# A hybrid layer's attention: the sum of exponentials by the tensor engine, value products in 65 columns, negated scores, and memory scores with 67 rows

## The chip, the core and the metric

The kernel runs on one core of a Trainium2 chip. The metric is the device time of one execution in microseconds (us). The core has a tensor engine (PE, whose weight loads are shown apart as PEld), a vector engine (DVE), a scalar engine (ACT), GpSimd (POOL) and a queue that issues DMAs (SP). PE writes its products to PSUM; POOL has no way to read PSUM.

## The reference, cut to what is computed

```python
D_MODEL, SEQ, HEAD_DIM, FOX_HEADS, MEM_HEADS, N_MEM = 1024, 2048, 64, 8, 4, 256

def fox_attention(q, k, v, logf):            # (B, H, S, 64), causal
    F = jnp.cumsum(logf, axis=-1)
    ...
    logits = einsum('bhqd,bhkd->bhqk', qi, k) * scale
    logits = logits + Fi[..., None] - F[:, :, None, :]
    logits = jnp.where(causal, logits, -1e30)
    p = jax.nn.softmax(logits, axis=-1)
    return einsum('bhqk,bhkd->bhqd', p, v)

def memory_attention(q, k, v):               # every query reads 256 memory tokens
    p = jax.nn.softmax(einsum('bhqd,bhmd->bhqm', q, k) * scale, axis=-1)
    return einsum('bhqm,bhmd->bhqd', p, v)

def reference(x, mem, ...):
    h = rms_norm(x, norm_g)
    u_a, g_a, q_b, k_b, v_b, f_b, g_b, q_m, g_m = split_cols(h @ w_in)
    y_a = pool_mixer(u_a, w_pool, pool_scale)
    y_b = fox_attention(rms_norm(q_b), rms_norm(k_b), v_b, log_sigmoid(f_b + b_f))
    y_m = memory_attention(rms_norm(q_m), rms_norm(k_m), v_m)
    mixed = concatenate([y_a * silu(g_a), y_b * silu(g_b), y_m * silu(g_m)])
    return x + mixed @ w_out
```

## The kernel before

The layer is cut into 16 units `n`: four groups `p` of heads (two forgetting-attention heads, one memory head, 64 pooled columns each) by four blocks `j` of 512 queries. For each unit PE first makes the input projection (`pa`, `pb` tiles, line 711), then the attention. At the end comes the output projection (`po`, also line 711). All operands are pairs of fp16 numbers, a high and a low part, so that one product takes three matmuls.

Attention of one head goes through these steps, with the queries on the partitions:

- `scores` (line 1113): q times k into a PSUM tile `qk` of 1024 columns, two matmuls per piece, line 1135 with the high parts and line 1140 with both parts. In the forgetting heads the first has 67 rows: 64 of the head, and three that carry the forget sums, against three rows of constants in `Q`. In the memory head (`h == 2`) it has 64 rows. Line 1138 adds the causal mask.
- `soften` (line 1144): DVE takes each row's largest score (line 1156) and its negative (line 1159); ACT makes the exponentials `p` and, through `accum_out`, their sum per row (line 1168; the second instruction is an ACTIVATION_READ_ACCUMULATOR).
- `weights` (line 1179): the factor of each part of the keys. There are two parts (`g` 0 and 1, of 1024 keys each) for `j` of 2 and 3, and one otherwise and in the memory head. POOL, ACT and DVE work on tiny tiles of up to 8 columns here, ending in a reciprocal of the sum.
- `halves` (line 1212): `p` as a high half `ph` (a cast, on ACT at line 1221 or DVE at line 1218) and a low half (a subtraction, line 1225, on DVE or POOL), and a DMA transpose to `pt` (line 1231), which puts the keys on the partitions. There are 336 such transposes.
- `weigh` (line 1236): for each block of 128 queries by 128 keys two matmuls into `pv`, of 128 columns (line 1260: high half by low and high part of the values) and 64 columns (line 1261: low half by high part), each with its own weight load.
- `gather`, `part`, `finish` (lines 1270 to 1317): DVE adds the two 64-column halves of `pv` (line 1277), scales by the factor (line 1311 four times per head, or 1300 and 1306 with two parts) and multiplies into the gate.

What sets the order is the class `Order`: a clock with a plain model of the engines (`COST`, and the costs that each step yields or gives to `use`). Each step runs when the model says that its operands are there; `sooner` picks the engine that would be done first. So one changed cost or step moves instructions everywhere, and which engine makes a high or a low half is decided anew. On the chip each engine then runs its instructions in this order. PSUM has two `qk` tiles and two `pv` tiles; seven subpieces may lie between scores and weighing (`DEEP`).

Of the kernel before, what the change touches and what calls it, by code (L numbers as in the profile page):

```python
# [10 lines left out]
F32 = mybir.dt.float32  # L11
F16 = mybir.dt.float16
# [22 lines left out]
NEG = -1e30  # L35
# [12 lines left out]
class Order:  # L48
    """Program order.  Processes are generators; each yields the tensor engine's time of what it has
    just emitted, or a negative time to be left alone for that long.  The clock follows a plain model  # L50
    of the engines, so that every engine's queue is filled in the order in which operands become ready."""
# [23 lines left out]
    def use(self, eng, n, fixed=None):  # L75
        """accounts for an instruction that has been emitted; returns when others see its result"""
# [34 lines left out]
    def claim(self, place):  # L111
        """waits for what has been reserved"""
# [30 lines left out]
    def merged(self, *streams):  # L143
        """Interleaves generators of given cost; each runs from fraction f0 to f1 of the whole."""
# [16 lines left out]
    def pair(self, lead, follow, lag):  # L161
        """Runs two generators of (unit, cost) on the tensor engine; follow's unit is kept lag behind lead's."""
# [23 lines left out]
def units(gen, start, total, span=1.0):  # L186
    """pairs each cost of gen with how far it has come, from start to start + span"""
# [11 lines left out]
class Layer:  # L199
    DEEP = 7  # score pieces in flight between the two products of the attention  # L200
# [1090 lines left out]
    def finish(self, n, h, head):  # L1291
# [23 lines left out]
        if g:  # L1315
            o.give(ft)
# [312 lines left out]
```

## Time and profile before

| what | value |
|---|---|
| device time, median of 3 runs | 1102.77 us (1100.82 to 1104.7) |
| span of the profiled execution, first to last instruction | 1095.0 us |
| busy: PE, DVE, ACT, POOL | 999.5, 852.6, 608.4, 468.3 us |
| granted PE clock, mean of the span | 0.981 of full |

The profile gives the span of its execution and no other time of it; the median of the runs is 7.8 us longer than that span. The chain of waits goes back from the last instruction, at each step to what released it. A busy PE may still be waiting inside, since matmuls overlap: how far apart two matmuls start tells more than how long one is said to take.

### The profile page before, as it was taken

To read this page: it belongs to the slowest core of one execution; us is meant where nothing else is said; L and a number is where in the kernel's file an instruction comes from. 1 tells how busy PE (TensorE), PEld (TensorE's weight loads), DVE (VectorE), ACT (ScalarE), POOL (GpSimd) and SP (SyncE) were. 2 spreads that over 40 slices of the span, in tenths; PEclk is the share of its full clock that TensorE was granted. 3 is DMA by queue.
4 is the path that set the end of the run, shared out by engine and by line. 5 is a ranking of instruction groups with operands and counts; after the bars stand their busy time and mean duration, and the time that the engine had idled before them with its cause. 6 is when DMAs were issued, how large, how long until landed. Compare 5 with 4: busy or idle time off the path is not lost.

```text
span 1095.0 us, 21836 instructions
## 1 busy us (share of the span) xinstructions
PE 999.5 (91%) x7477; PEld 588.6 (54%) x7477; DVE 852.6 (78%) x2059; ACT 608.4 (56%) x1867; POOL 468.3 (43%) x554
## 2 busy tenths in 40 slices
PE   6799899979899999998999898989899979999998
PEld 3356555546556555555565555555556644554443
DVE  6977887688998997987987979889978797872111
ACT  4776666576757466666664667476556564440000
POOL 5643453254545454545435446564535463220000
PEclk9899998999999999999999999999999999999999
DMA  9999999999999998998999969999989799998531
GB/s 273 229 220 211 219 247 252 254 149 177 180 208 205 216 209 189 188 169 165 206 205 222 205 148 206 199 216 203 194 227 214 158 169 254 226 234 213 196 104 48
DMA packets 485694, 219.20 MB, mean 200 GB/s; under 512 B 442128, under 2 KB 450256, under 8 KB 484560
## 3 DMA queue, kind: packets, MB, share of 16 engines
q1 hardware_dynamic: 485440, 217.81, 91.4%
q8 instruction: 58, 0.95, 0.4%
q14 instruction: 52, 0.43, 0.1%
q10 hardware_dynamic: 144, 0.01, 0.0%
HBM read 84.23 MB, written 25.26 MB: 100 GB/s over the span
## 4 chain that ended last, share of the span: by engine, by line
PE 40%; DVE 26%; DMA 16%; ACT 7%; issue 6%; POOL 4%; SPq 2%; ACTq 0%; POOLq 0%; DVEq 0%
PE po L711 14%; DMA pt<-ph 12%; PE pa L711 10%; DVE mx L1156 5%; PE pb L711 5%; DVE ph L1225 3%; ACT p L1168 3%; PE q L1135 2%; PE q L1140 2%; PE pv L1260 2%; DVE gate L1311 2%; DVE ph L1218 2%; DMA xx<-k 2%; POOL rr L966 1%; DVE hy L1277 1%
## 5 line engine op out<-in xcount | busy, mean ns | idle before, releaser
L1168 ACT ACTIVATE p<-q,nm 128x512 f32<-128x512 f32 (+3 forms) x384 | 228.8, 602 | 168.0 <-DVE nm L1159 105.0
L711 PEld LDWEIGHTS <-x 128*128 128x128 f16 x2304 | 215.9, 99 | 136.6 <-issue 4.5
L1225 POOL TENSOR_TENSOR ph<-p,ph 128x512 f16<-128x512 f32 (+3 forms) x153 | 174.2, 1144 | 218.5 <-ACT ph L1221 101.7
L711 PE MATMUL pa<-ah,x 128*128 128x512 f16 x768 | 250.3, 382 | 2.0 <-DVE z L941 2.0
L1156 DVE TENSOR_REDUCE mx<-q 128x1 f32<-128x128 f32 (+2 forms) x192 | 171.1, 905 | 10.4 <-PE q L1140 10.2
L1260 PE MATMUL pv<-v,pt 128*128 128x128 f16 x1088 | 132.4, 221 | 35.2 <-DMA pt<-ph 34.8
L711 PE MATMUL po<-aho,om 128*128 128x512 f16 x512 | 160.3, 382 | 0.0
L1260 PEld LDWEIGHTS <-pt 128*128 128x128 f16 x1216 | 110.5, 98 | 74.0 <-DMA pt<-ph 57.0
L711 PE MATMUL pa<-al,x 128*128 128x512 f16 x384 | 147.0, 383 | 0.0
L711 PE MATMUL pb<-bh,x 128*128 128x256 f16 x768 | 144.5, 275 | 2.5 <-ACT sq L932 1.0
L1221 ACT CAST ph<-p 128x512 f16<-128x512 f32 (+3 forms) x198 | 113.3, 585 | 38.9 <-DMA pt<-ph 28.9
L1225 DVE TENSOR_TENSOR ph<-p,ph 128x512 f16<-128x512 f32 (+3 forms) x183 | 125.4, 694 | 7.5 <-ACT ph L1221 5.2
L1135 PE MATMUL q<-k,q 67*128 67x512 f16 (+2 forms) x320 | 111.3, 350 | 19.4 <-ACT p L1168 17.6
L1261 PE MATMUL pv<-v,pt 128*128 128x64 f16 x1088 | 124.2, 193 | 0.0
L711 PEld LDWEIGHTS <-om 128*128 128x128 f16 x768 | 73.7, 99 | 84.5 <-issue 3.0
L1261 PEld LDWEIGHTS <-pt 128*128 128x128 f16 x1216 | 107.6, 98 | 20.3 <-issue 1.1
L966 POOL TENSOR_TENSOR rr<-ss,mhalf 128x10 f32<-128x10 f32 x32 | 64.6, 2018 | 121.8 <-DVE ss L961 106.7
L1140 PE MATMUL q<-k,q 128*128 128x512 f16 (+2 forms) x320 | 111.0, 349 | 0.0
L711 PE MATMUL pb<-bl,x 128*128 128x256 f16 x384 | 105.5, 275 | 0.0
L711 PE MATMUL po<-alo,om 128*128 128x512 f16 x256 | 97.8, 382 | 0.0
L711 PEld LDWEIGHTS <-xx 128*128 128x128 f16 x720 | 70.0, 100 | 51.5 <-issue 7.4
L1493 DVE SCALAR_TENSOR_TENSOR xo<-po,So_p,xo 128x512 f32<-128x512 f32 x32 | 23.9, 748 | 87.1 <-PE po L711 87.1
(245 smaller groups left out, 1762.7 us busy)
## 6 DMA issues: line engine op xcount, KB each, us to landing
x<-xd SPq DMA_DIRECT2D x48, 512.0 KB, 5.6
xrx<-in_x SPq DMA_DIRECT2D x16, 512.0 KB, 4.4
xd<-xx SPq DMA_DIRECT2D x16, 512.0 KB, 9.4
md<-mt SPq DMA_DIRECT2D x32, 256.0 KB, 3.5
om<-md SPq DMA_DIRECT2D x8, 1024.0 KB, 6.7
xo<-in_x SPq DMA_DIRECT2D x16, 512.0 KB, 3.8
out_dram<-xo SPq DMA_DIRECT2D x32, 256.0 KB, 3.9
w0a<-in_w_a SPq DMA_DIRECT2D x12, 512.0 KB, 5.2
```

The lines of the kernel that those rows point to most:

```text
L711: nc.tensor.matmul(out, rows, r[kt][:, :ncol], start=(kt == 0 and i == 0), stop=(kt == KT - 1 and i == 2))
L966: nc.gpsimd.tensor_tensor(rr, ss, self.mhalf[:, 0:10].rearrange("p (a b) -> p a b", b=5), op=ALU.pow)
L1135: nc.tensor.matmul(out, q1, kb, start=bank not in used, stop=False, **kw)
L1140: nc.tensor.matmul(out, q2, ka, start=False, stop=True, **kw)
L1156: nc.vector.tensor_reduce(mx[:, g, i:i + 1], qk[:, off:off + w], axis=AX.X, op=ALU.max)
L1168: nc.scalar.activation(p32[:, at:at + w], qk[:, off:off + w], AF.Exp, bias=nm[:, g, i:i + 1], accum_out=head["ls"][:, g, part, i:i + 1])
L1218: nc.vector.tensor_copy(hl[:, :w], p32[:, :w])
L1221: nc.scalar.copy(hl[:, :w], p32[:, :w])
L1225: (nc.vector if eng == "V" else nc.gpsimd).tensor_tensor(hl[:, w:2 * w], p32[:, :w], hl[:, :w], op=ALU.subtract)
L1260: nc.tensor.matmul(pv[:, i, :], ph, v, start=start and b == 0, stop=False, **kw)
L1261: nc.tensor.matmul(pv[:, i, HD:], pl, v[:, HD:], start=False, stop=end and b == nb - 1, **kw)
L1493: nc.vector.scalar_tensor_tensor(xr[:, t, :], pj, self.So, xr[:, t, :], op0=ALU.mult, op1=ALU.add)
```

## The change

The exponentials' sum is no longer made by ACT. Each values tile gets one more column, a constant of 2^14 behind the high part (`VW` is 132 columns per head of which 129 are used), so that PE's product of exponentials and values gives the sum in column 64. The value product of a block is now three matmuls into the same 65 columns: high half by [high part, constant], high half by low part (64 columns), low half by [high part, constant]. So `gather`, which added two halves, and `weights` are gone. `pv` has 65 columns per query block in place of 128.

The scores are negated (the gains and the constant rows of `Q` change sign), so DVE takes the smallest, and ACT's exponential has a scale of -1. The second part of the keys uses the smaller of the two parts' values, so that only the first part needs a factor, one `exp` of a difference (`al`). The memory scores read three more rows, which are zero in the keys.

At the end of a head DVE takes the reciprocal of column 64 and multiplies by it, straight from PSUM where there is one part. The product with the gate is always POOL's. `hy` has three buffers in place of two; some costs of the model change (the exponential's, a value block's); the scratch for dynamic DMA descriptors is set to 1024 bytes.

```diff
-            v = kv.tile([P, 4, 2, P], F16, name=f"v{i}")
+            self.V.append(kv.tile([P, 4, 2, VW], F16, name=f"v{i}"))
...
+        for v in [*self.V, self.Vm]:
+            nc.gpsimd.memset(v[:, :, :, 2 * HD:2 * HD + 1], ONE)
...
+            nc.gpsimd.memset(self.Km[HD:HD + 3, 0], 0.0)
...
-        r = HD + 3 if h < 2 else HD
+        r = HD + 3
...
-                nc.vector.tensor_reduce(mx[:, g, i:i + 1], qk[:, off:off + w], axis=AX.X, op=ALU.max)
+                nc.vector.tensor_reduce(mn[:, g, i:i + 1], qk[:, off:off + w], axis=AX.X, op=ALU.min)
...
-        nc.vector.tensor_scalar(nm[:, g, i0:i1], mx[:, g, i0:i1], -1.0, LN_P, op0=ALU.mult, op1=ALU.add)
+        if g:
+            nc.vector.scalar_tensor_tensor(
+                nm[:, 1, i0:i1], mn[:, 1, i0:i1], LN_P, nm[:, 0, i0:i1], op0=ALU.add, op1=ALU.min
+            )
+        else:
+            nc.vector.tensor_scalar(nm[:, 0, i0:i1], mn[:, 0, i0:i1], LN_P, None, op0=ALU.add)
...
-                    p32[:, at:at + w], qk[:, off:off + w], AF.Exp, bias=nm[:, g, i:i + 1], accum_out=head["ls"][:, g, part, i:i + 1]
-                t = o.use("A", 1.1 * w + 140)
+                nc.scalar.activation(p32[:, at:at + w], qk[:, off:off + w], AF.Exp, bias=nm[:, g, i:i + 1], scale=-1.0)
+                t = o.use("A", 1.0 * w + 180)
...
-            yield from self.weights(n, h, g, head)
+        if g and i1 == 4:
+            al = head["al"] = self.sm.tile([P, 4], F32, tag="al", bufs=3, name=f"al{n}{h}")
+            nc.gpsimd.tensor_tensor(al, nm[:, 1, :], nm[:, 0, :], op=ALU.subtract)
+            yield from o.at(o.use("G", 0, 0.3))
             nc.scalar.activation(al, al, AF.Exp)
...
-                nc.tensor.matmul(pv[:, i, :], ph, v, start=start and b == 0, stop=False, **kw)
-                nc.tensor.matmul(pv[:, i, HD:], pl, v[:, HD:], start=False, stop=end and b == nb - 1, **kw)
+                hi = v[:, HD:2 * HD + 1]
+                nc.tensor.matmul(pv[:, i, :], ph, hi, start=start and b == 0, stop=False, **kw)
+                nc.tensor.matmul(pv[:, i, 0:HD], ph, v[:, 0:HD], start=False, stop=False, **kw)
+                nc.tensor.matmul(pv[:, i, :], pl, hi, start=False, stop=end and b == nb - 1, **kw)
...
-                    yield 0.0856 * (2 - b % 2)
+                    yield 0.0885 * (2 - b % 2)
...
     def part(self, n, h, head):
...
+        yield from o.until(lambda: "scaled" in head)
+        nc.vector.tensor_tensor(y, pv, head["al"].unsqueeze(2).broadcast_to([P, 4, HD + 1]), op=ALU.mult)
...
     def finish(self, n, h, head):
...
+            nc.vector.tensor_tensor(y, y, pv, op=ALU.add)
...
+        nc.vector.reciprocal(rs, src[:, :, HD])
+        nc.vector.scalar_tensor_tensor(
+            y[:, :, 0:HD], src[:, :, 0:HD], 2.0 ** -29 * ONE, rs.unsqueeze(2).broadcast_to([P, 4, HD]), op0=ALU.mult, op1=ALU.mult
+        )
...
+        for u in range(2):
+            gate = head["gates"][u][0][:, :, c0:c0 + HD]
+            nc.gpsimd.tensor_tensor(gate, gate, y[:, 2 * u:2 * u + 2, 0:HD], op=ALU.mult)
```

In numbers of instructions, over the whole program: PE gets 1216 more matmuls and as many more weight loads. The low halves (`ph<-p,ph`) stand 221 times on DVE and 115 on POOL, where it was 183 and 153; the high halves 168 times on ACT and 168 on DVE, where it was 198 and 138. The gate products stand 96 times on POOL, where 128 multiplications of 64 columns stood on DVE (line 1311) and 24 and 8 of 128 columns on POOL and DVE (line 1306).

On PE, at the first memory head's values (`vm` are the memory's values, `pt` the transposed halves), the program before has, for one block:

```order
L1140 LDWEIGHTS q_124
L1140 MATMUL q_1233<-k_113,q_124 128x512
L1260 LDWEIGHTS pt_1155
L1260 MATMUL pv_1244<-vm,pt_1155 128x128
L1261 LDWEIGHTS pt_1155
L1261 MATMUL pv_1244<-vm,pt_1155 128x64
```

And the changed program, at the same place:

```order
L1144 LDWEIGHTS q_124
L1144 MATMUL q_1210<-k_113,q_124 128x384
L1238 LDWEIGHTS pt_1179
L1238 MATMUL pv_1229<-vm,pt_1179 128x65
L1239 LDWEIGHTS pt_1179
L1239 MATMUL pv_1229<-vm,pt_1179 128x64
L1240 LDWEIGHTS pt_1179
L1240 MATMUL pv_1229<-vm,pt_1179 128x65
```

The block has a third pair of load and matmul, and the same weights are loaded twice running.

On DVE, where the third unit's memory head ends (`hy` is the sum of its values, `al` its factor), the program before has:

```order
L1277 TENSOR_REDUCE hy_2859<-pv_2823 128x256
L1054 TENSOR_TENSOR flf_2772<-flf_2772,faz_2771 128x32
L1218 CAST ph_2898<-p_2839 128x512
L984 SCALAR_TENSOR_TENSOR kk<-raw_2485,kk 128x2x64 x2
L1311 SCALAR_TENSOR_TENSOR gate_1427<-hy_2859,al_2739,gate_1427 128x64 x2
L1311 SCALAR_TENSOR_TENSOR gate_1715<-hy_2859,al_2739,gate_1715 128x64 x2
L1218 CAST ph_2924<-p_2866 128x512
```

The changed program has, at the end of the same head:

```order
L1160 TENSOR_REDUCE mn_2672<-q_2849 128x1
L1168 TENSOR_SCALAR nm_2673<-mn_2672 128x1
L1280 RECIPROCAL rs_2888<-pv_2823 128x4
L1282 SCALAR_TENSOR_TENSOR hy_2889<-pv_2823,rs_2888 128x4x64
L1195 CAST ph_2899<-p_2884 128x512
L1195 CAST ph_2918<-p_2886 128x512
```

A reduction and four scalings are replaced by a small reciprocal and one multiplication, and casts of high halves follow directly. On POOL the changed program has, after that head:

```order
L1202 TENSOR_TENSOR ph_2845<-p_2821,ph_2845 128x512
L1384 TENSOR_TENSOR mh_2847<-gate_1054,mh_2847 128x2x256
L1291 TENSOR_TENSOR gate_1442<-gate_1442,hy_2889 128x2x64
L1291 TENSOR_TENSOR gate_1737<-gate_1737,hy_2889 128x2x64
L1202 TENSOR_TENSOR ph_2959<-p_2908,ph_2959 128x512
```

The two gate products, which DVE had at line 1311, now stand on POOL between low halves (`ph`).

## Rows read from the trace of the kernel before

**Rows 1.** The page's part 1: busy us, share of the span, instructions.

```profile
PE 999.5 (91%) x7477; PEld 588.6 (54%) x7477; DVE 852.6 (78%) x2059; ACT 608.4 (56%) x1867; POOL 468.3 (43%) x554
```

**Rows 2.** The chain of waits by line, shares of the span.

```profile
PE po L711 14%; DMA pt<-ph 12%; PE pa L711 10%; DVE mx L1156 5%; PE pb L711 5%; DVE ph L1225 3%; ACT p L1168 3%; PE q L1135 2%; PE q L1140 2%; PE pv L1260 2%; DVE gate L1311 2%; DVE ph L1218 2%; DMA xx<-k 2%; POOL rr L966 1%; DVE hy L1277 1%
```

**Rows 3.** A stretch's busy us of PE, PEld, DVE, ACT, POOL; clock, DMA share, GB/s.

```profile
350.00:400.00 50.00, 46.10 (x359) 27.98 (x357) 47.03 (x122) 29.64 (x102) 24.71 (x24) 1.00 0.98 224
```

**Rows 4.** Waits: who waited for whom, us in total, times, longest.

```profile
PE pv L1260 <- DMA pt<-ph: 37.8, 41, 2.2
PE q L1135 <- ACT p L1168: 17.6, 22, 2.7
...
POOL gate L1306 <- DVE hy L1300: 33.4, 21, 18.0
```

**Rows 5.** The DMA queue's own waits.

```profile
SPq L1231 <- POOL ph L1225: 80.5, 54, 10.3
```

**Rows 6.** Timeline of PE in memory scores: start us, us, what.

```profile
638.35 0.28 PE L1135 MATMUL q<-km,q 64*128 64x256 f16 x1
638.56 0.28 PE L1140 MATMUL q<-km,q 128*128 128x256 f16 x1
638.78 0.28 PE L1135 MATMUL q<-km,q 64*128 64x256 f16 x1
```

**Rows 7.** Timeline of PE: scores with 67 rows, four value blocks, projection.

```profile
604.07 0.38 PE L1140 MATMUL q<-k,q 128*128 128x512 f16 x1
604.29 0.38 PE L1135 MATMUL q<-k,q 67*128 67x512 f16 x1
604.51 0.22 PE L1138 MATMUL q<-mask,identb 128*128 128x128 bf16 x1
...
604.78 0.22 PE L1260 MATMUL pv<-vm,pt 128*128 128x128 f16 x1
604.84 0.19 PE L1261 MATMUL pv<-vm,pt 128*128 128x64 f16 x1
604.86 0.22 PE L1260 MATMUL pv<-vm,pt 128*128 128x128 f16 x1
...
605.12 0.27 PE L711 MATMUL pb<-bh,x 128*128 128x256 f16 x1
```

**Rows 8.** Groups by line and shape: count, busy us, mean ns, idle before.

```profile
L1260 PEld LDWEIGHTS <-pt 128*128 128x128 f16 x1216 | 110.5, 98 | 74.0 <-DMA pt<-ph 57.0 <-issue 0.6
```

**Rows 9.** Groups by line and shape on DVE that the change takes out.

```profile
L1277 DVE TENSOR_REDUCE hy<-pv 128x256 f32<-128x512 f32 x64 | 43.7, 682 | 6.9 <-PE pv L1261 6.9
L1311 DVE SCALAR_TENSOR_TENSOR gate<-hy,al,gate 128x64 f32<-128x64 f32 x128 | 38.4, 361 | 0.1
L1300 DVE SCALAR_TENSOR_TENSOR hy<-hy,al,hy 128x64 f32<-128x64 f32 x64 | 20.8, 384 | 0.1
L1208 DVE TENSOR_SCALAR al<-rs 128x4 f32<-128x4 f32 x32 | 15.3, 477 | 1.1
```

**Rows 10.** The group of line 1156 with 256 columns, read from PSUM.

```profile
L1156 DVE TENSOR_REDUCE mx<-q 128x1 f32<-128x256 f32 x16 | 6.6, 414 | 0.0
```

**Rows 11.** The group of ACT's sums.

```profile
L1168 ACT ACTIVATION_READ_ACCUMULATOR p<-q,nm 128x1 f32 x384 | 78.2, 204 | 0.0
```

**Rows 12.** Timeline of ACT: one such sum and the next exponential.

```profile
425.72 0.19 ACT L1168 ACTIVATION_READ_ACCUMULATOR p<-q,nm 128x1 f32 x1
425.81 0.46 ACT L1168 ACTIVATE p<-q,nm 128x256 f32<-128x256 f32 x1
```

**Rows 13.** The page's groups of low halves (line 1225) and high halves (line 1221).

```profile
L1225 POOL TENSOR_TENSOR ph<-p,ph 128x512 f16<-128x512 f32 (+3 forms) x153 | 174.2, 1144 | 218.5 <-ACT ph L1221 101.7
...
L1221 ACT CAST ph<-p 128x512 f16<-128x512 f32 (+3 forms) x198 | 113.3, 585 | 38.9 <-DMA pt<-ph 28.9
L1225 DVE TENSOR_TENSOR ph<-p,ph 128x512 f16<-128x512 f32 (+3 forms) x183 | 125.4, 694 | 7.5 <-ACT ph L1221 5.2
```

**Rows 14.** The group of gate products on POOL.

```profile
L1306 POOL TENSOR_TENSOR gate<-gate,hy 128x128 f32<-128x128 f32 x24 | 12.5, 521 | 33.4 <-DVE hy L1300 33.4
```

More of the change, by code (lines that the diff above doesn't have):

```diff
@@ L202 @@
         "x": 3, "st": 4, "w": 2, "b": 2, "pj": 2, "qk": 2, "pv": 2, "p32": 3, "ph": 5, "pt": 6, "qkr": 2, "qsq": 2,
[L203 removed]
+        "gate": 7, "z": 3, "kk": 1, "Q": 2, "cs": 2, "pw": 1, "hy": 3, "band": 1, "rx": 4, "cs2": 2, "early": 3, "late": 2, "scaled": 1,
     }
@@ L1244, in weigh @@
             tk = yield from o.take("pv")
-            head["pv"][g] = (self.ps_pv.tile([P, 4, P], F32, tag="pv", name=f"pv{n}{h}{g}"), tk)
+            head["pv"][g] = (self.ps_pv.tile([P, 4, HD + 1], F32, tag="pv", name=f"pv{n}{h}{g}"), tk)
             start = True
@@ L1293, in finish @@
         g = max(head["pv"])
-        al, c0 = head["al"], (0, HD, 3 * HD)[h]
-        y, yt = yield from self.gather(n, h, g, head)
+        c0 = (0, HD, 3 * HD)[h]
+        pv, tk = head["pv"][g]
+        rs = self.sm.tile([P, 4], F32, tag="rs", name=f"rs{n}{h}")
         if g:
             yield from o.until(lambda: "first" in head)
-            first, ft = head["first"]
-            for q in range(4):
-                nc.vector.scalar_tensor_tensor(y[:, q], y[:, q], al[:, 1, q:q + 1], first[:, q], op0=ALU.mult, op1=ALU.add)
-                t = o.use("V", HD)
-            yield from o.at(t)
-            for u in range(2):
-                gate = head["gates"][u][0][:, :, c0:c0 + HD]
-                eng = o.sooner(2 * HD, "V", "G")
-                (nc.vector if eng == "V" else nc.gpsimd).tensor_tensor(gate, gate, y[:, 2 * u:2 * u + 2], op=ALU.mult)
-                t = max(t, o.use(eng, 2 * HD))
-        else:
-            for q in range(4):
-                gate = head["gates"][q // 2][0][:, q % 2, c0:c0 + HD]
-                nc.vector.scalar_tensor_tensor(gate, y[:, q], al[:, 0, q:q + 1], gate, op0=ALU.mult, op1=ALU.mult)
-                t = o.use("V", HD)
+            y, yt = head["first"]
+            nc.vector.tensor_tensor(y, y, pv, op=ALU.add)
+            yield from o.at(o.use("V", 320))
+            o.give(tk)
+            src = y
+        else:
+            yt = yield from o.take("hy")
+            y = self.sm.tile([P, 4, HD + 1], F32, tag="hy", bufs=self.BUFS["hy"], name=f"hy{n}{h}")
+            src = pv
+        nc.vector.reciprocal(rs, src[:, :, HD])
+        o.use("V", 0, 0.17)
+        nc.vector.scalar_tensor_tensor(
+            y[:, :, 0:HD], src[:, :, 0:HD], 2.0 ** -29 * ONE, rs.unsqueeze(2).broadcast_to([P, 4, HD]), op0=ALU.mult, op1=ALU.mult
+        )
+        yield from o.at(o.use("V", 310))
+        if not g:
+            o.give(tk)
+        t = 0.0
+        for u in range(2):
+            gate = head["gates"][u][0][:, :, c0:c0 + HD]
+            nc.gpsimd.tensor_tensor(gate, gate, y[:, 2 * u:2 * u + 2, 0:HD], op=ALU.mult)
+            t = o.use("G", 2 * HD, 0.5)
         yield from o.at(t)
         o.give(yt)
-        if g:
-            o.give(ft)
         self.done.add(("y", n, h))
@@ L1352, in attention @@
                 head = {
-                    "mx": self.sm.tile([P, 2, 4], F32, tag="mx", bufs=3, name=f"mx{n}{h}"),
+                    "mn": self.sm.tile([P, 2, 4], F32, tag="mn", bufs=3, name=f"mn{n}{h}"),
                     "nm": self.sm.tile([P, 2, 4], F32, tag="nm", bufs=3, name=f"nm{n}{h}"),
                     "pv": {}, "box": {}, "subs": subs, "count": count, "gates": gates, "last": h == 1,
-                    "flat": [sub for group in subs for _, sub in group], "pieces": len(pieces), "parts": defaultdict(int),
-                    "ls": self.sm.tile([P, 2, 2, 4], F32, tag="ls", bufs=3, name=f"ls{n}{h}"),
+                    "flat": [sub for group in subs for _, sub in group],
                 }
```

81 lines of the change are left out of this document (20 added, 61 removed).

## The prediction

> **What bounds the kernel now.** I read the page's busy shares first, then the chain of waits, then who waited for whom, then stretches and timelines. PE is busy 91% of the span, DVE 78%, ACT 56% and POOL 43% [rows 1]. So the first question is what PE does in its busy time, and the second what it waits for. The chain of waits is mixed: PE's lines lead it, but transposes hold 12% of it, and several DVE lines 2 to 5% each [rows 2]. Two waits of PE belong to attention: 37.8 us in 41 waits for the transposed halves `pt`, and 17.6 us in 22 waits for an exponential that frees a score tile [rows 4]. Together that is 55.4 us, the most that a faster supply can give back. Where attention is thick, DVE is busy 47.03 of 50 us, more than PE's 46.10 [rows 3]: there DVE, in its fixed order, is what supplies PE late. I therefore see a PE kernel whose losses come from a nearly full DVE upstream, and, behind it, from DMAs.
>
> **The change part by part.**
>
> *Memory scores.* A memory pair is one matmul with 64 rows and one with 128, of 256 columns each; the next pair starts 0.43 us later, at 638.78 after 638.35 [rows 6]. Matmuls with 67 and 128 rows in turn show no such thing: 512 columns start 0.22 us apart both ways, 604.07 to 604.29 to 604.51 [rows 7], which is 0.11 for 256 columns and 0.22 for a pair. So each switch between 64 and 128 rows costs about 0.1 us. With 67 rows, three of them zero in the keys, the pair should take 0.22. There are 16 units with 4 query tiles: 64 x 0.21 = 13.4 us of PE time less. I take all of it; the other end is nothing, if the switch has another cause than the rows.
>
> *Value products.* Four blocks take 0.34 us (604.78 to 605.12), 0.085 each for 192 columns, of which the 128 columns take 0.06 and the 64 columns with their own weight load 0.02 to 0.03 [rows 7]. The new block has 194 columns in three matmuls, each with its load: at the same rate per column 0.086. Over 1216 blocks [rows 8] that is +1.1 us. Lower bound: 0, as columns don't fall. Upper bound: each short matmul as slow as the one of 128 columns, 3 x 0.06 - 0.085 = 0.095, which is +115 us. I take +1.1, since the 64-column row is of the same kind and nearly the same size.
> A rule of the Trainium skill speaks against this edit. Its page "TensorE: Matmul & The Clock Gate", section "Back-to-back issue gap", gives about 81 ns per matmul for a sustained stream of load and matmul pairs with 128 columns. An estimate from that page: a third pair per block would add 81 ns x 1216 = 98 us, and the kernel would get slower. The trace here does not agree: it has 60 ns for 128 columns and under 30 for 64 [rows 7], and the measurement decides.
>
> *DVE.* What goes: 43.7 us of adding halves, 38.4 and 20.8 of scalings in pieces of 64 columns, 15.3 of factors [rows 9], 118.2 together. The reciprocals stay, 48 of them. What comes: 48 multiplications of 256 elements and 32 operations of 260, most with an operand in PSUM. The nearest row reads 256 columns from PSUM in 414 ns [rows 10]: 80 x 0.414 = 33.1 us. The ends are 384 ns, a scaling of 64 columns, and 682 ns, a reduction of 512 [rows 9]: 30.7 to 54.6 us. So 85 us less (64 to 88). The planner then moves work to DVE: 38 low halves at 694 ns, 26.4 us, and 30 high halves, at no more than a low half's 694 ns, 20.8 us [rows 13]. DVE should end some 38 us lighter, near 815.
>
> *ACT.* The 384 sum instructions are recorded with 78.2 us [rows 11], but the next exponential starts 0.09 us after one began, at 425.81 after 425.72 [rows 12]; so they hold ACT for 35 to 78 us. The 30 high halves that leave it are 17.6 us [rows 13]. Each score tile is also freed a little earlier. The exponential itself keeps its shape; its scale of -1 I cost at nothing.
>
> *POOL.* It gets 72 gate products more, 72 x 0.521 = 37.5 us [rows 14], and loses 38 low halves, 38 x 1.144 = 43.5 us [rows 13], and the tiny work on factors. That is even, or a bit less. The eight memsets at the start cost at most 8 x 0.521 = 4 us by the same row, under the first loads and projections; if that cover were gone, it would be 4 us.
>
> *A new wait.* With two key parts, DVE's scaling of part 0 waits for the factor, which exists only after the last scores of part 1. Behind it on DVE stand the next row minima and halves, and PE waits for the `pv` tile if both are held. The planner places the scaling behind the factor, so I take 0. A wait can't gain, so that is the lower end; the upper is one stall of 1.6 us (as long as POOL's mean wait at a head's end, 33.4 over 21 [rows 4]) in each of the 16 heads with two parts, 26 us. The third `hy` buffer, the wider values tile and the smaller scratch add no instruction; I cost them at nothing.
>
> *What this is worth to PE.* Lightening an engine is worth what it holds of the chain. Line 1311 holds 2% (22 us) and line 1277 1% (11 us) [rows 2]. What replaces the 118.2 us is 33.1, or 28%, so 72% of 33, that is 24 us, may go. ACT's line holds 3%, and a sixth of that (5 us) is the sums; I leave those 5 for the halves that move onto DVE. The bounds are 0 (what is next late is a landing transpose) and 55.4 (all waits of PE gone).
>
> **The sum.** -13.4 + 1.1 - 24 = -36.3 us. Against the profiled span of 1095.0 that is 1058.7; the median of the runs is 7.8 above the span, and I keep that: 1066.5, forecast **1066 us**. With all waits gone it would be 1102.8 - 12.3 - 55.4 = 1035; with none gone 1090.
>
> **Rivals.**
>
> *Only the switches go (1090).* The 336 transposes are unchanged, they hold 12% of the chain [rows 2], and the DMA share is 0.98 in the thick stretch [rows 3]. If the DMAs are the limit there, PE comes earlier to the same landings and the 55.4 us stay. Against it: the DMA queue itself waits 80.5 us for POOL's halves [rows 5], so it is not simply full.
>
> *Nothing moves (1102).* As above, and the 12.3 us are also given back in waits for transposes.
>
> *67 rows still switch (1080).* Then the change does not do what its memory part says: 1066.5 + 13.4. The forgetting heads' rows speak against it [rows 7].
>
> *POOL stalls, slower (1109).* The gate products stand in POOL's queue in front of low halves, and wait for DVE's end of a head. Today POOL waits 33.4 us there, 21 times, 1.6 us each, up to 18.0 [rows 4]. With 48 heads it could be 48 x 1.6 = 77 us, 43 more. If all of that reaches PE through late halves, 1066.5 + 43 = 1109; it decides from 36 us on. Against it: POOL idles 218.5 us before its low halves already [rows 13], and it gets fewer of them.
>
> *Short matmuls are paced by their loads, slower (about 1180).* The upper bound above: 1066.5 + 114. From 36 us, or 30 ns a block, it outweighs the rest. The 64-column row speaks against it.
>
> **How the numbers follow.** Chances: forecast 0.58 (its own range 1035 to 1085), only the switches 0.22, 67 rows still switch 0.05, nothing 0.05, POOL 0.07, loads 0.03. A change under about 0.3%, some 3 us, can't be told from none. Faster: 0.58 + 0.22 + 0.05 = 0.85; same 0.05; slower 0.10. The range 1034 to 1092 takes in the forecast's bounds and the case of the switches alone, and leaves out about 0.15 to 0.2.
>
> **What would show it.** In the changed profile memory pairs should start 0.22 us apart, value blocks 0.085 to 0.09. No sums should stand on ACT. DVE should be busy near 815 us, with the multiplication at a head's end near 0.4 us. PE's two waits should fall from 55.4 to about 30 us; if they stay and the DMA share with them, the first rival holds. Waits of POOL's gate products for DVE well above 33.4 us, with PE's waits for `pt` grown, would be the POOL rival. The forecast is wrong at its root if value blocks take over 0.11 us.

## The result, and the profile after

The changed kernel takes 1104.2 us, median of 20 runs (1096.4 to 1108.4), the kernel before 1099.1 us, median of 20 (1093.6 to 1106.1), on the same chip. The ratio is 1.0052, 95% interval 1.0032 to 1.0072. It is slower by half a per cent, where 1066 us was forecast; the time lies outside the range of 1034 to 1092.

The profiled execution has a span of 1102.8 us at a mean granted clock of 0.977 (before 0.981). The page's busy shares and its chain of waits by line:

```profile
PE 1000.0 (91%) x8693; PEld 600.3 (54%) x8693; DVE 817.5 (74%) x1895; ACT 562.1 (51%) x1453; POOL 433.0 (39%) x484
PE po L714 12%; DMA pt<-ph 12%; PE pa L714 4%; PE pb L714 3%; DVE mn L1160 3%; DVE ph L1202 2%; DVE ph L1195 1%; PE pv L1238 1%; PE q L1139 1%; PE q L1144 1%; PE pv L1240 1%; PE pv L1239 1%; SPq L1208 1%; POOL ph L1202 1%; DVE qq L998 1%
```

The stretch of [rows 3] (busy us of PE, PEld, DVE, ACT, POOL; clock, DMA share, GB/s):

```profile
350.00:400.00 50.00, 48.03 (x460) 31.36 (x458) 42.82 (x113) 27.72 (x84) 25.73 (x30) 1.00 1.01 221
```

DVE, ACT and POOL are lighter by 35, 46 and 35 us than in [rows 1], DVE as forecast (about 815); ACT's 46 is short of the 53 to 96 that the prediction's parts come to (35 to 78 for the sums, 17.6 for the halves). In the thick stretch DVE fell from 47.03 to 42.82 us. PE's busy time stayed at 1000. (The chain of this trace breaks off half way, so its shares aren't compared.) The waits, as in [rows 4] (engine and line, waiting for whom: us, times, longest):

```profile
POOL ph L1202 <- DVE ph L1195: 148.3, 46, 15.5
POOL gate L1291 <- DVE hy L1282: 105.6, 27, 22.9
PE pv L1238 <- DMA pt<-ph: 59.6, 62, 3.2
ACT ph L1198 <- DMA pt<-ph: 58.2, 44, 5.8
DVE ph L1195 <- DMA pt<-ph: 30.8, 21, 4.4
PE q L1139 <- ACT p L1175: 8.8, 12, 2.1
```

And the DMA queue's own, as in [rows 5]:

```profile
SPq L1208 <- PE pv L1240: 77.3, 83, 2.5
SPq L1208 <- POOL ph L1202: 29.9, 21, 11.2
```

PE's two waits went from 55.4 to 68.4 us: the one for `pt` grew from 37.8 to 59.6. The DMA queue waits 29.9 us for POOL's halves where it waited 80.5, and 36.8 for DVE's low halves where it waited 26.8; for PE, whose value products free the `pt`, it waits 77.3 us where it waited 48.8:

```profile
SPq L1231 <- PE pv L1261: 48.8, 53, 1.9
SPq L1231 <- DVE ph L1225: 26.8, 24, 3.1
...
SPq L1208 <- DVE ph L1202: 36.8, 25, 8.7
```

(The first two lines are of the kernel before, the last of the changed one.) ACT and DVE now wait 89.0 us together for a `ph` that a transpose still reads, 37.8 before. The supply seems to have turned from late halves to late transposes.

PE's timeline (start us, us, what), where it answers to [rows 6] and [rows 7]:

```profile
696.82 0.28 PE L1139 MATMUL q<-km,q 67*128 67x256 f16 x1
696.93 0.27 PE L1144 MATMUL q<-km,q 128*128 128x256 f16 x1
697.04 0.27 PE L1139 MATMUL q<-km,q 67*128 67x256 f16 x1
...
607.76 0.19 PE L1238 MATMUL pv<-vm,pt 128*128 128x65 f16 x1
607.79 0.20 PE L1239 MATMUL pv<-vm,pt 128*128 128x64 f16 x1
607.83 0.19 PE L1240 MATMUL pv<-vm,pt 128*128 128x65 f16 x1
607.86 0.19 PE L1238 MATMUL pv<-vm,pt 128*128 128x65 f16 x1
...
608.04 0.19 PE L1238 MATMUL pv<-vm,pt 128*128 128x65 f16 x1
```

And the groups by line and shape at a head's end (count, busy us, mean ns, idle before):

```profile
L1282 DVE SCALAR_TENSOR_TENSOR hy<-pv,rs 128x256 f32<-128x256 f32 x32 | 13.6, 424 | 1.2
L1282 DVE SCALAR_TENSOR_TENSOR hy<-hy,rs 128x256 f32<-128x256 f32 x16 | 10.9, 683 | 0.5
L1291 POOL TENSOR_TENSOR gate<-gate,hy 128x128 f32<-128x128 f32 x96 | 50.6, 549 | 105.6 <-DVE hy L1282 105.6
```

Memory pairs start 0.22 us apart, as forecast. Three value blocks take 0.28 us (607.76 to 608.04), 0.093 each and not 0.086. The multiplication takes 0.424 us, as forecast, in the 32 heads with one part, which read PSUM; in the 16 with two parts, where it reads `hy`, it takes 0.683.

### The profile page after: what moved, and what is told of

Its sections match the earlier page's. It is cut to its first block, busy times and chain, and to the rows that moved or that the text cites. A ratio compares the mean times of both kernels' runs of the same rounds, so it can differ in the third digit from the quotient of the medians.

```text
span 1102.8 us, 23610 instructions
## 1 busy us (share of the span) xinstructions
PE 1000.0 (91%) x8693; PEld 600.3 (54%) x8693; DVE 817.5 (74%) x1895; ACT 562.1 (51%) x1453; POOL 433.0 (39%) x484
## 3 DMA queue, kind: packets, MB, share of 16 engines
q1 hardware_dynamic: 485440, 217.81, 91.4%
## 4 chain that ended last, share of the span: by engine, by line
PE 23%; DMA 12%; DVE 11%; issue 2%; SPq 1%; ACT 1%; POOL 1%; DVEq 0%; ACTq 0%; POOLq 0%
PE po L714 12%; DMA pt<-ph 12%; PE pa L714 4%; PE pb L714 3%; DVE mn L1160 3%; DVE ph L1202 2%; DVE ph L1195 1%; PE pv L1238 1%; PE q L1139 1%; PE q L1144 1%; PE pv L1240 1%; PE pv L1239 1%; SPq L1208 1%; POOL ph L1202 1%; DVE qq L998 1%
## 5 line engine op out<-in xcount | busy, mean ns | idle before, releaser
L1175 ACT ACTIVATE p<-q,nm 128x512 f32<-128x512 f32 (+3 forms) x384 | 216.3, 601 | 168.0 <-DVE nm L1168 79.6
L1202 POOL TENSOR_TENSOR ph<-p,ph 128x512 f16<-128x512 f32 (+3 forms) x115 | 134.6, 1175 | 259.2 <-DVE ph L1195 148.3
L1238 PE MATMUL pv<-v,pt 128*128 128x65 f16 x1088 | 130.8, 194 | 56.5 <-DMA pt<-ph 56.1
L1160 DVE TENSOR_REDUCE mn<-q 128x1 f32<-128x128 f32 (+2 forms) x192 | 170.7, 902 | 6.8 <-PE q L1144 6.6
L1202 DVE TENSOR_TENSOR ph<-p,ph 128x512 f16<-128x512 f32 (+3 forms) x221 | 159.5, 732 | 18.1 <-ACT ph L1198 16.5
L1238 PEld LDWEIGHTS <-pt 128*128 128x128 f16 x1216 | 114.3, 99 | 105.0 <-DMA pt<-ph 89.9
L714 PE MATMUL pb<-bh,x 128*128 128x256 f16 x768 | 140.8, 273 | 1.6 <-DVE v L925 1.5
L1198 ACT CAST ph<-p 128x512 f16<-128x512 f32 (+3 forms) x168 | 97.2, 586 | 72.5 <-DMA pt<-ph 58.2
L1239 PE MATMUL pv<-v,pt 128*128 128x64 f16 x1088 | 130.3, 194 | 0.0
L1240 PE MATMUL pv<-v,pt 128*128 128x65 f16 x1088 | 129.9, 195 | 0.0
L1239 PEld LDWEIGHTS <-pt 128*128 128x128 f16 x1216 | 113.9, 98 | 16.8 <-issue 0.8
L1240 PEld LDWEIGHTS <-pt 128*128 128x128 f16 x1216 | 114.2, 98 | 0.0
L1195 DVE CAST ph<-p 128x512 f16<-128x512 f32 (+3 forms) x168 | 77.2, 468 | 35.3 <-DMA pt<-ph 30.8
```

The costliest lines, as they stand in the source:

```text
L714: nc.tensor.matmul(out, rows, r[kt][:, :ncol], start=(kt == 0 and i == 0), stop=(kt == KT - 1 and i == 2))
L1160: nc.vector.tensor_reduce(mn[:, g, i:i + 1], qk[:, off:off + w], axis=AX.X, op=ALU.min)
L1175: nc.scalar.activation(p32[:, at:at + w], qk[:, off:off + w], AF.Exp, bias=nm[:, g, i:i + 1], scale=-1.0)
L1195: nc.vector.tensor_copy(hl[:, :w], p32[:, :w])
L1198: nc.scalar.copy(hl[:, :w], p32[:, :w])
L1202: (nc.vector if eng == "V" else nc.gpsimd).tensor_tensor(hl[:, w:2 * w], p32[:, :w], hl[:, :w], op=ALU.subtract)
```

## The experiments

Ratios are to the kernel before, run beside each on the same chip, with 95% intervals; 0.1% is 1.1 us. The runs came on five chips, so what is compared between them are ratios, not times. "Old order" means that the planner's accounting was kept, so that every instruction that isn't itself changed stands where it stood in the kernel before. The expectations call the engines TensorE (PE), VectorE (DVE), ScalarE (ACT), GpSimd (POOL) and SyncE (SP). Theory 1 is that the transposes land late, theory 2 that POOL stalls, theory 3 that the planner counts on landings too early; the theory of the order is that another order alone costs or gains time.

| run | what | ratio | interval |
|---|---|---|---|
| (after) | the change | 1.0052 | 1.0032 to 1.0072 |
| e3 | after, gate products on DVE | 1.0044 | 1.0019 to 1.0070 |
| e4, e8 | after, landings planned 1.5, 3.0 us later | 0.9957, 1.0063 | 0.9930 to 0.9984, 1.0039 to 1.0087 |
| e7 | before, landings planned 1.5 us later | 1.0036 | 1.0006 to 1.0066 |
| e1 | before, 67 rows, planner told | 1.0136 | 1.0105 to 1.0168 |
| e6 | before, planner told, nothing else | 1.0241 | 1.0198 to 1.0283 |
| e5 | before, 67 rows, old order | 0.9965 | 0.9935 to 0.9995 |
| e2 | before, value product split, old order | 1.0083 | 1.0053 to 1.0112 |
| e11 | before, planner's wait 0.21 for 0.20 us | 1.0132 | 1.0094 to 1.0171 |
| e10 | after, nudged as e6 | 1.0094 | 1.0060 to 1.0128 |
| e12 | after, nudged as e11 | 1.0025 | 0.9999 to 1.0051 |
| e9 | the whole change, old order | 0.9936 | 0.9913 to 0.9959 |
| e17 | e9 with ACT's sums back | 0.9997 | 0.9972 to 1.0022 |
| e13 | e9, 8 buffers `ph` | 0.9945 | 0.9920 to 0.9969 |
| e14 | e9, 8 buffers `pt` | 0.9918 | 0.9888 to 0.9948 |
| e15 | before, 8 of both | 1.0000 | 0.9980 to 1.0020 |
| e16 | after, 8 of both | 1.0005 | 0.9978 to 1.0032 |
| e18 | e9, half the reloads of `x` | 0.9762 | 0.9733 to 0.9792 |

### Is it POOL? (e3)

```diff
-            nc.gpsimd.tensor_tensor(gate, gate, y[:, 2 * u:2 * u + 2, 0:HD], op=ALU.mult)
+            nc.vector.tensor_tensor(gate, gate, y[:, 2 * u:2 * u + 2, 0:HD], op=ALU.mult)
```

> The changed kernel, with the 96 gate products at the heads' ends on VectorE, right behind the multiplication that they need, in place of GpSimd; everything else in the same order. GpSimd's 105.6 us of waits for VectorE at that place go, and VectorE works some 20 to 30 us more. Theory 2 (GpSimd's stall delays the low halves, and these TensorE): 15 to 30 us faster than the changed kernel, TensorE's waits for `pt` (59.6 us) fall by as much. Theory 1 (late landings) and theory 3 (the order's optimism): within 4 us of the changed kernel, up to 5 slower for VectorE's extra work.

POOL's 105.6 us of waits at that place are gone; DVE does the 96 products in 28.7 us, with 0.3 us of idle time before them. DVE's busy time grew by only 10.2 us (827.7), as its other instructions took less. The group in e3:

```profile
L1291 DVE TENSOR_TENSOR gate<-gate,hy 128x128 f32<-128x128 f32 x96 | 28.7, 340 | 0.3
```

The ratio is 1.0044 against 1.0052, and PE's wait (of e3's list of waits) is what it was:

```profile
PE pv L1238 <- DMA pt<-ph: 59.5, 61, 3.3
```

So the POOL rival is out as the cause of the loss (some gain may still hide behind DVE's 10 us), although both of its signs (POOL's waits well above 33.4, PE's waits for `pt` grown) stood in the trace.

### Is it the plan's optimism? (e4, e8, e7)

```diff
-MARGIN = 0
+MARGIN = 1.5
```

> The changed kernel, whose planner counts every transposed tile `pt` as there 1.5 us later than it did (its own margin, 0 so far), so that value products are written later into TensorE's order. Theory 3 (the plan is too optimistic about the landings, so TensorE stands at a value product while other work is ready): TensorE's waits for `pt` fall from 59.6 to below 35 us and the time falls by 10 to 25 us. Theory 1 (the transposes themselves are the limit): the waits move to score tiles and `pt` buffers and the time stays within 5 us or grows. Theory 2 (GpSimd's stall): within 5 us, since the stall stays.

> The changed kernel with the planner's margin at 3.0 us in place of 1.5. Theory 3 (waits for landings come from the plan's optimism): TensorE's waits for `pt`, 59.6 us at margin 0 and 39.2 at 1.5, fall to 25 or less; the time is at or below 1096.6, down to 1085. Theory of the order: waits and time scatter, 1090 to 1110, with no trend in the margin. Theory 1 (transposes as the limit): as at 1.5 or slower, waits moved to score tiles.

> The kernel before, whose planner counts every transposed tile `pt` as there 1.5 us later, as the changed kernel did above (with 8 to 10 us gained). Theory 3 (the planner of both kernels is too optimistic about landings): TensorE's waits for `pt` fall from 37.8 to 25 us or less and the time falls by 5 to 12 us, so that the changed kernel stays behind. Theory of the order (only a better draw of the order in the changed kernel): anywhere from 10 us faster to 15 us slower.

In the changed kernel the wait for `pt` falls with the margin, 59.6, 39.2, 20.9 us, as theory 3 has it. The time doesn't follow: 1.0052, 0.9957, 1.0063. In the kernel before, the wait falls from 37.8 to 32.5 us, and it gets 0.36% slower. The lines of e4, e8 and e7:

```profile
PE pv L1238 <- DMA pt<-ph: 39.2, 40, 4.3
PE pv L1238 <- DMA pt<-ph: 20.9, 21, 2.6
PE pv L1260 <- DMA pt<-ph: 32.5, 38, 2.8
```

Two thirds of PE's wait at the value products can be planned away, and the time comes back at another place. What differs between such runs beside the waits is the order of everything.

### The 67 rows, and the order (e1, e6, e5)

```diff
-        r = HD + 3 if h < 2 else HD
+        r = HD + 3
...
+            nc.gpsimd.memset(self.Km[HD:HD + 3, 0], 0.0)
             nc.vector.tensor_copy(self.Km[0:HD, 0], self.Km[HD:P, 1])
-            yield from o.at(o.use("V", 256))
+            yield from o.at(max(o.use("V", 256), o.use("G", 1024)))
```

e1 has all of this, e6 the last two lines alone, e5 all but them.

> The kernel before, with only the memory scores changed: 67 rows, three of them zero in the memory's keys. The pairs should start 0.22 us apart in place of 0.43, 64 x 0.21 = 13.4 us of TensorE's time less, by every theory. Theory 1 (late landings: the saved time of TensorE turns into waits for the transposed halves `pt`): the kernel gains 0 to 4 us, and TensorE's waits for `pt` grow from 37.8 to 47 us or more. Theory 2 (GpSimd's queue stalls at the heads' ends, in the changed kernel only) and theory 3 (only the order of the changed kernel is worse): the full 13 us come out, near 1086.

> The kernel before with 64 rows and not one instruction added, removed or changed; the planner only accounts for 2 us of GpSimd's time at the memory's keys (as it did in the first run of the 67 rows), and so lays out the same work in another order. Theory of the order: 10 to 30 us slower than before for this alone, with TensorE's waits for `pt` near 58 in place of 37.8 us. By theories 1 and 2 an order that is as good a plan as the other moves the time by no more than 3 us.

> The kernel before with 67 rows in the memory scores, and this time every engine's instructions in exactly the order of the kernel before (the one new memset is not accounted for by the planner). In the run of the 67 rows before this one the planner had accounted for the memset and laid out all engines in another order. With the order kept nothing is done later than before, so TensorE can only gain. Theory of the order (that run's 15 us loss is the new order's, and 13 us of switches are real): 5 to 13 us faster than the kernel before, 1087 to 1095, TensorE's waits for `pt` between 37.8 and 50. Theory 1 (late landings take it all back): within 3 us of before, waits up by 13. That the 67 rows cost time themselves: slower here too, by up to 15 us.

e1 came out 1.36% slower, which no theory had. e6 explains it. It computes the same operations as the kernel before in the layout of e1, and is 2.4% slower, 26 us. More than half of PE's instructions stand at another place than before, and the planner gave DVE ten instructions more, and ACT and POOL five fewer each. PE's wait for `pt` in e6 (37.8 before), and the page's busy shares:

```profile
PE pv L1260 <- DMA pt<-ph: 50.2, 65, 2.5
```

```profile
PE 1009.1 (90%) x7477; PEld 590.3 (53%) x7477; DVE 858.1 (77%) x2069; ACT 606.8 (54%) x1862; POOL 462.7 (41%) x549
```

Of the 23.3 us by which e6's span is longer (1118.3 against 1095.0), 9.6 are busy time of PE for the same matmuls, at a mean granted clock of 0.971 against 0.981, and 13.7 are PE's idle time.

In the old order (e5) the 67 rows gain 0.35%, 3.9 us (0.5 to 7.1), between what theory 1 (within 3) and the theory of the order (5 to 13) gave. In the nudged order they gain (e1 against e6) 1.0136 / 1.0241, that is 1.0% or 11 us (6 to 17). PE's busy time fell by the forecast 13 us in e5 (first its busy shares, then its wait for `pt`):

```profile
PE 986.5 (91%) x7477; PEld 589.4 (54%) x7477; DVE 852.4 (78%) x2059; ACT 606.9 (56%) x1867; POOL 463.9 (43%) x555
```

```profile
PE pv L1261 <- DMA pt<-ph: 36.1, 44, 1.9
```

So the switch costs PE what the timelines said, 0.1 us each. The Trainium skill, "TensorEngine Tiling (Array Packing)", section "Key Properties", says that a change of tiling mode drains TensorE; the trace agrees in so far as the time goes with the 64 rows, but no run shows the drain itself. How much of that reaches the end depends on the order.

### The split value product (e2)

```diff
-                nc.tensor.matmul(pv[:, i, :], ph, v, start=start and b == 0, stop=False, **kw)
+                nc.tensor.matmul(pv[:, i, HD:], ph, v[:, HD:], start=start and b == 0, stop=False, **kw)
+                nc.tensor.matmul(pv[:, i, 0:HD], ph, v[:, 0:HD], start=False, stop=False, **kw)
```

> The kernel before, with only the value product of 128 columns issued as two of 64 columns, each with its own weight load; same result, same order, 1216 more matmuls. If three short matmuls take the time of their columns, a block stays at 0.085 us and the time is unchanged within 3 us. If the changed kernel's 0.090 to 0.093 us per block is the price of the split itself, TensorE works 6 to 10 us longer; theory 1 (late landings) gives 0 to 4 us of that to the time, since TensorE's waits shrink by the rest, theories 2 and 3 give it whole.

The same 192 columns in three matmuls instead of two cost 0.83%, 9.1 us (5.8 to 12.3), or 7.5 ns for each of the 1216 blocks. PE's busy time grew by 9.9 us (from 999.5 to 1009.4), so all of it reached the end, as theories 2 and 3 had it. In the timeline matmuls of 64 columns start 0.03 us apart, so a block comes to 0.09 us:

```profile
608.20 0.20 PE L1260 MATMUL pv<-vm,pt 128*128 128x64 f16 x1 [1.15 <-DMA pt<-ph]
608.24 0.19 PE L1261 MATMUL pv<-vm,pt 128*128 128x64 f16 x1
608.27 0.19 PE L1262 MATMUL pv<-vm,pt 128*128 128x64 f16 x1
608.30 0.19 PE L1260 MATMUL pv<-vm,pt 128*128 128x64 f16 x1
```

### More orders of both kernels (e10 to e12)

```diff
-            yield from o.at(max(o.use("V", 256), o.use("G", 1024)))
+            yield from o.at(max(o.use("V", 256), o.use("G", 2048)))
...
-SEM = 0.2
+SEM = 0.21
```

> The changed kernel with nothing changed but the planner's account of GpSimd at the memory's keys, 2 us more, the nudge that cost the kernel before 2.4%. Theory of the order: another draw, anywhere between 1090 and 1130; if orders are all alike for this kernel, within 3 us of 1105.

> The kernel before with no instruction changed, the planner's time from an engine to who waits for it at 0.21 us in place of 0.20. Theory of the order (the order of the kernel before is a good draw among many): 8 to 30 us slower than 1099. If the first nudge was one unlucky case: within 4 us.

> The changed kernel with the same nudge, 0.21 us in place of 0.20. Theory of the order: between 1090 and 1130. If, order for order, the change is a gain that only the old kernel's good draw hides, then this is faster than the old kernel with the same nudge, by 5 to 25 us; if the change is no gain, the two are within 5 us.

With the same nudge on either side, the changed kernel is the faster one three times out of three, by 0.8 to 1.4%: 1.0094 against 1.0241 (the memory's keys), 1.0025 against 1.0132 (0.21 us), 0.9957 against 1.0036 (e4, e7). Only in their own orders is it the slower one. Of the four orders of the kernel before, its own is the fastest, the others lie 0.4 to 2.4% above; the changed kernel's five orders reach from -0.4 to +0.9%.

### The whole change in the old order (e9, e17)

e9 has the arithmetic of the change and the planner's accounting of before, for instance at a head's end:

```diff
+        nc.vector.reciprocal(rs, src[:, :, HD])
+        nc.vector.scalar_tensor_tensor(
+            y[:, :, 0:HD], src[:, :, 0:HD], 2.0 ** -29 * ONE, rs.unsqueeze(2).broadcast_to([P, 4, HD]), op0=ALU.mult, op1=ALU.mult
+        )
         yield from o.at(o.use("V", 512))
```

> All of the changed kernel's arithmetic (67 rows, three value matmuls of 65, 64 and 65 columns, no sums on ScalarE, one scaling at a head's end, gate products on GpSimd), laid out in the order of the kernel before: the planner keeps that kernel's accounting, so SyncE's queue, all other products and all halves stand as before, and only the changed instructions differ. (In 8 of the 16 heads with two key parts the first part's factor is not there yet at the place where the old kernel added halves; there VectorE copies the part out and GpSimd scales it, as it did before.) Theory of the order (the change is good work in a bad order): faster than before, 1065 to 1092; with the split at +9 and the 67 rows at -4 measured, the lighter VectorE and ScalarE would be worth what is left, -24 by the forecast, so about 1080. Theory 1 (the relief does not reach TensorE in any order): 1099 + 9 - 4 = 1104, within 4 us, TensorE's waits for `pt` at 38 or above.

> The changed work in the old order (0.9936 of the kernel before), with the sums of the exponentials put back on ScalarE, where nothing reads them; no instruction moves. ScalarE works 35 to 78 us more. If ScalarE's relief was the gain: 8 to 12 us slower than without the sums, at about the old kernel's time. If VectorE's was, as the prediction had it (it gave ScalarE 5 us and let the halves eat them): within 3 us of 0.9936.

e9 is 0.64% faster than the kernel before, 7.0 us (4.5 to 9.6), at 1093.7 us, just short of what the theory of the order gave (at most 1092) and far from its 1080; theory 1's 1104 is further off, though its sign came (PE's wait for `pt` at 55.5, where 38 or above was expected). By 1.0052 / 0.9936 the change's own order costs 1.2%, 12.8 us (9 to 16). That price takes in the halves that the planner moves to DVE, which e9 leaves where they were (DVE is busy 801.8 us in e9 and 817.5 after), and the part that POOL scales in 8 heads of e9. With the sums back on ACT (e17) the gain is gone: they are worth 0.61%, 6.7 us (3 to 10), where the prediction gave ACT 5 us and took them away again for halves that move to DVE. The busy shares of e9, then of e17:

```profile
PE 996.4 (91%) x8693; PEld 596.2 (55%) x8693; DVE 801.8 (73%) x1827; ACT 573.8 (53%) x1483; POOL 469.8 (43%) x530
PE 997.5 (91%) x8693; PEld 596.6 (55%) x8693; DVE 802.2 (73%) x1827; ACT 605.6 (55%) x1867; POOL 469.6 (43%) x530
```

If the parts add up, which no run shows, the split at +9.1 and the rows at -3.9 leave, out of -7.0, 12.2 us for the lighter engines: 6.7 of ACT's sums and some 5.5 (by difference, give or take 6) of DVE's 51 us.

Where DVE's relief stopped shows in the chain of waits by engine, first of e5, then of e9 (the order is the same), and in e9's list of waits:

```profile
PE 34%; DVE 29%; DMA 18%; ACT 6%; issue 6%; POOL 4%; SPq 3%; ACTq 0%; DVEq 0%; POOLq 0%
```

```profile
PE 38%; DMA 27%; DVE 17%; POOL 5%; issue 5%; SPq 4%; ACT 3%; POOLq 0%; DVEq 0%; ACTq 0%
```

```profile
PE pv L1255 <- DMA pt<-ph: 55.5, 61, 3.4
ACT ph L1215 <- DMA pt<-ph: 48.2, 41, 3.3
...
DVE ph L1212 <- DMA pt<-ph: 24.3, 23, 2.2
...
PE q L1139 <- ACT p L1177: 7.3, 11, 4.0
```

DVE's part fell by 12 points, and DMA's rose by 9 (in e13 below, with the same time, DMA's part is 19%, so DMA's rise is less sure than DVE's fall). PE's wait for landings rose from 36.1 to 55.5 us.

### Buffers, or the DMA queue? (e13 to e16, e18)

```diff
-        hl = self.pp.tile([P, 2 * TB], F16, tag="ph", bufs=self.BUFS["ph"], name=f"ph{n}{h}{c}")
+        hl = self.pp.tile([P, 2 * TB], F16, tag="ph", bufs=8, name=f"ph{n}{h}{c}")
...
-        T = self.pp.tile([P, 8, P], F16, tag="pt", bufs=self.BUFS["pt"], name=f"pt{n}{h}{c}")
+        T = self.pp.tile([P, 8, P], F16, tag="pt", bufs=8, name=f"pt{n}{h}{c}")
```

> The changed work in the old order (1093.7), with 8 buffers `ph` for the halves in place of 5; the planner still counts 5, so no instruction moves. The halves' waits for a `ph` that a transpose still reads (48.2 us on ScalarE, 24.3 on VectorE) must nearly vanish. Theory P (the relief of VectorE and ScalarE is lost in waiting for `ph`): 8 to 15 us faster, TensorE's waits for `pt` fall from 55.5 us by as much. Theory T (the transposes behind them are what is late; halves that come earlier only queue for SyncE): within 3 us of 1093.7, SyncE's waits for halves fall and TensorE's stay.

> The changed work in the old order, with 8 buffers `pt` for the transposed halves in place of 6, planner as before, no instruction moves. SyncE's waits for TensorE at a transpose (52.9 us) should fall below 25, so transposes start earlier. Theory B (the ring is closed at `pt`: TensorE waits for a landing that waited for TensorE): 8 to 20 us faster, TensorE's waits for `pt` down by as much. Theory T (the transposes' own time on the queue is the limit): within 3 us.

> The kernel before, same work and order, with 8 `ph` and 8 `pt` (and the smaller scratch of the changed kernel, to make room). If buffers hold it too: 5 to 15 us faster than before. If VectorE is what holds it, as the prediction had it: within 3 us, since its halves come late and find buffers free.

> The changed kernel in its own order, with 8 `ph` and 8 `pt`. If its order costs time because value products stand before their landings can be there and buffers are held meanwhile: 10 to 20 us faster than 1105, TensorE's waits for `pt` (59.6 us) below 45. If the order's price is in the order itself, whatever the buffers: within 4 us of 1105.

With 8 `ph` the 72 us of waits of ACT and DVE vanish from the list, and the time stays (0.9945). SP's waits for POOL's halves did not fall as expected; they went from 73.4 to 82.0 us. So what ACT and DVE no longer wait did not reach the transposes. With 8 `pt`, SP's wait for PE falls from 52.9 to 40.4 us (below 25 was expected), and the time by 0.2%, which can't be told from none. The kernel before gains nothing (1.0000). The changed kernel in its own order goes from 1.0052 to 1.0005, some 5 us, which lies between the two expectations (10 to 20, or within 4), and PE's wait for `pt`, expected below 45, stays at 61.5 us; the intervals just touch, so this part stays open.

```diff
+            if t:
+                ts = o.use("S", 1 << 19)
+            else:
+                ts = self.copy(X[:, t], self.xd[b][:, t], 1 << 19)
```

> The changed work in the old order, with 24 of the 48 reloads of normalised inputs `x` left out (512 KB each; in passes 1 to 3 the second 128 rows of a block are computed from the first 128 rows' data, so those outputs are of other rows); same instructions on all engines otherwise. At some 2 to 3 us of queue each that is 50 to 70 us less for the DMA queue. Theory T (the transposes wait for the queue, whose share is near full): TensorE's waits for `pt` (55.5 us) fall by 15 to 30 and the time by as much. If the queue is not the limit (it waits for GpSimd's halves, 73 us, as before): within 4 us of the same kernel with all reloads.

The chain by engine and the DMA queue on e18's page (packets, MB, share of 16 engines), and PE's two waits:

```profile
PE 44%; DVE 21%; DMA 20%; issue 4%; ACT 4%; POOL 4%; SPq 2%; DVEq 0%; ACTq 0%; POOLq 0%
q1 hardware_dynamic: 481984, 205.23, 90.7%
```

```profile
PE pv L1260 <- DMA pt<-ph: 33.6, 39, 2.8
PE q L1144 <- ACT p L1182: 10.0, 11, 3.8
```

The same queue on e9's page:

```profile
q1 hardware_dynamic: 485440, 217.81, 93.2%
```

So it moves 12.6 MB less. (Its working time, share times span, is no good measure of that: 1017 us in e9 and 972 in e18, but 981 in e17, which moves the same 217.81 MB as e9:)

```profile
q1 hardware_dynamic: 485440, 217.81, 89.8%
```

The time falls by 1.75%, 19 us, and PE's wait for `pt` by 21.9 us, in the same order. So fewer transfers in front of the transposes are worth that much to e9. SP also issues 24 transfers less; this run can't tell the transfers from their issue. The kernel before was not run with fewer reloads, so it isn't shown that these 19 us are the relief of DVE that went missing, and not time that the queue costs both kernels.

## Why the prediction was wrong, point by point

Four terms of the sum failed, by like amounts. Between the forecast change of -36.3 us and the +5.8 that the terms come to as measured lie 42 us: 12.8 of the order, 11.8 of the relief, 9.5 of the switches and 8.0 of the split. None of them alone would have saved the forecast; even in the old order the change takes 1093.7 us.

- **The order was priced at nothing, and it cost 12.8 us.** The prediction counted what the planner moved ("The planner then moves work to DVE", 38 and 30 halves) but took the new layout as equal to the old one. The step that failed is this one that isn't there. The kernel before sits in a good order; three other layouts of its operations cost 0.4, 1.3 and 2.4%. Laid out in the old order the change is faster, by 0.64%.
- **"What this is worth to PE" was mis-sized, 24 against about 12.** The chain's share of two DVE lines, times 72%, took it that a share of the chain comes out in full. In the old order some 5.5 us (give or take 6) came of DVE and 6.7 of ACT. So "a PE kernel whose losses come from a nearly full DVE upstream" doesn't hold: DVE lost 51 us, and most of that did not reach the end. The bound that the prediction itself named ("what is next late is a landing transpose") fits what the traces show: the chain went from DVE to DMA, PE's two waits rose from 55.4 to 62.8 us in e9, and in that order fewer transfers brought them furthest down, to 43.6 (e18). The Trainium skill, "Perfetto Trace Analysis", section "Identifying the Most-Contended Engine", would have one work first on the engine with the highest occupancy (TensorE is to be judged by other measures); here DVE, at 78%, lost 51 us of work for about 5.5, while 24 transfers fewer brought 19. The same section says that occupancy misleads for DMA; here the queue's busy time for the same transfers was 981 us in e17 and 1017 in e9.
- **ACT was netted to zero** ("I leave those 5 for the halves that move onto DVE"). Its sums were worth 6.7 us (3 to 10), about half of the relief.
- **Value blocks: right in kind, short in size.** 0.086 was forecast and 0.093 came; +1.1 us became +9.1. The 64-column row was read as 0.02 to 0.03 and scaled by columns. At 0.03 for each matmul of 64 or 65 columns, three make 0.09. The prediction's own limit of 0.11 for "wrong at its root" was kept, and the rival of paced loads (1180) was far off.
- **The switches were right on PE and too large at the end.** The 13 us came out of PE's busy time (999.5 to 986.5) and 3.9 us out of the time. "I take all of it" is the step. In another order 11 us (6 to 17) came out, so how much of it is taken back seems to depend on the order.
- **The base was some 4 us too high.** The sum took "the median of the runs is 7.8 above the span", which sets the median of three runs against the span of another execution. In the runs on record an execution takes some 2 us more than its own span, and 20 runs of the kernel before have a median of 1099.1, not 1102.8. That shifts the forecast, not the change.
- **The loads** came as forecast on DVE (817.5 for 815; 0.424 for 0.4 us at a head's end, though 0.683 in the 16 heads with two parts). ACT lost 46 us where 53 to 96 was forecast; 16 of them are the moved halves, so the sums held it for some 30, below the 35 to 78. POOL got 35 us lighter where "even, or a bit less" stood.
- **The rivals.** "POOL stalls" (1109) showed its signs and was not the cause (e3). "Nothing moves" (1102) came nearest to the 1104.2 by luck: its terms are not those that were measured. It and "Only the switches go" named the right next limit, the DMAs; both lack the split, the order and the relief that did come.

The terms as measured: -3.9 (rows) + 9.1 (split) - 12.2 (lighter engines) = -7.0 in the old order, + 12.8 for the new order = +5.8, where the ratio gives +5.7. The -12.2 and the 12.8 are differences of runs, so the sum closes by construction. Why just this order is dearer was not found: POOL's stall at the gate products is excluded as the main part, 8 buffers of both kinds took some 5 us (1 to 9) off the time, and planning the landings later moved the waits and gave no trend. The mean granted clock of the kernel before is 0.981 in its own order, and lower in the three dearer ones (0.973 in e7, 0.969 in e11, 0.971 in e6). But among the orders of the changed kernel it doesn't sort the times: e4 has 0.968 and is faster than after with 0.977. Whether the lower clock makes the orders dear or follows from PE's waits in them isn't shown.

## What to carry to other kernels

Where a planner lays out the order, one edit is two changes: the work, and a new order of everything, and the second can be the larger. Keep the accounting and run the new work in the old order, and nudge the accounting with the old work; the two together give each its price, before a wait in the trace is believed as a cause. And a share of the chain of waits is worth at most what lies between it and the next late thing, here by all signs the DMA queue.

The version to keep is the change in the old order: e9 at 1093.7 us, 0.6% under the kernel before. With 8 `pt` (e14) it took 1089.9 us, 0.8% under, which can't be told from e9.

## What the runs showed of the hardware that was not expected

The same 192 columns in three matmuls with their loads cost the kernel 7.5 ns a block more than in two (e2), and matmuls of 64 and 65 columns start about 0.03 us apart. An accumulator read behind an exponential, recorded with 204 ns [rows 11], holds ACT for less: ACT's busy time differs by 31.8 us over 384 of them (605.6 in e17, 573.8 in e9), 83 ns each, and they cost the kernel 6.7 us.
